# ReLU and row sum on one core: own semaphores, wide instructions, three buffers of 64 KB per partition, and a first load split into 16 and 112 partitions

## Chip, cores, metric

One core of a Trainium2 chip. The metric is device time in microseconds (us); the spans in the profiles are 1.7 to 2.1 us shorter. ACT is the scalar engine, DVE the vector engine, SP the engine that issues the loads. A load (or the chunk of rows that it brings) has landed when the first instruction that waits for it starts. Ratios in this document are the mean time of one kernel's fast runs over the mean of the other's fast runs of the same rounds, so they are not quite the ratios of the medians that are quoted. A run that was timed once is compared with the median of the runs of before on the same chip; such runs carry only differences of several us.

## The reference

```
x: float32 [32, 512, 1024]
relu_x = np.maximum(x, 0)
return np.sum(relu_x, axis=-1)        # [32, 512]
```

That is 16,384 rows of 1,024 elements: 67.1 MB to read, 64 KB to write.

## The kernel before

Each of the 128 partitions gets 128 rows that lie together in memory (512 KB), so a load of 16 rows is 128 runs of 64 KB, 8.4 MB in all. Seven loads of 16 rows go through two buffers. After them come tail loads of 8, 4, 2 and 1 rows, and the last row in four pieces. Each row takes one instruction, on ACT or DVE in turn, which clamps and sums it.

```
big = 16
tail = [8, 4, 2, 1]
io_pool = ctx.enter_context(tc.tile_pool(name="io", bufs=2))
...
for j, cpd in enumerate(chunks):
    xt = io_pool.tile([P, cpd, D], fp32, tag="io", name=f"xt{j}")     # (cut: small tiles have own tags)
    nc.sync.dma_start(out=xt, in_=xv[:, m0 * D : (m0 + cpd) * D].rearrange(...))
    for c in range(cpd):
        ...
        elif (c % 2) == 0:
            act_op(xt[:, c, :], xt[:, c, :], m)       # activation Relu with accum_out
        else:
            dve_op(xt[:, c, :], xt[:, c, :], res[:, m : m + 1])   # tensor_scalar max, add, accum_out
```

The first load is issued ahead of the opening barrier (`EARLY = 1`).

## Time and profile before

| | before |
|---|---|
| median (first three runs) | 163.46 us (163.4 to 163.71) |
| span of the profiled run | 161.5 us |
| busy: DVE, ACT | 46%, 43% |
| 64 KB packet of a load, most of them | 2.42 us |
| first landing; distance of landings | 22.3 us; 19.4 us |

From the page of before: the span, the busy rows, the mean DMA rate and the chain of work that ended last.

```profile
span 161.5 us, 347 instructions
DVE 74.3 (46%) x134; ACT 69.0 (43%) x129; POOL 0.2 (0%) x4
...
DMA  8997997996997997997996997997997997999990
GB/s 308 471 503 308 487 487 308 503 503 292 503 503 308 487 503 325 471 519 308 471 519 296 487 503 325 471 503 341 454 503 341 454 503 308 430 438 406 406 359 22
...
DMA 79%; DVE 18%; SPq 1%; issue 0%; DVEq 0%
```

The chain is DMA. From the timeline of before, the first instruction on each of the first four loads (start in us, length in us, then the idle time before it and what ended it):

```profile
22.26 1.06 ACT L71 ACTIVATE xt<-xt 128x1024 f32<-128x1024 f32 x1 [20.20 <-DMA xt<-in_x_dram]
...
41.61 1.06 ACT L71 ACTIVATE xt<-xt 128x1024 f32<-128x1024 f32 x1 [10.92 <-DMA xt<-in_x_dram]
...
61.04 1.06 ACT L71 ACTIVATE xt<-xt 128x1024 f32<-128x1024 f32 x1 [11.01 <-DMA xt<-in_x_dram]
...
80.39 1.06 ACT L71 ACTIVATE xt<-xt 128x1024 f32<-128x1024 f32 x1 [10.92 <-DMA xt<-in_x_dram]
```

Landings are 19.4 us apart. The packet records in the trace say why. A 16-row load has 128 packets of 64 KB, eight for each of the 16 DMA engines. Sorted by start and taken in groups of 16, one packet per engine, the first groups are:

```
before: group  start us      took ns min/median/max   end us
        0      1.02-2.27     2547/3042/3236           3.97-4.98
        1      3.97-4.98     2418/2418/2472           6.39-7.40
        2      6.38-7.39     2418/2420/2467           8.80-9.81
        7     18.47-19.48    2418/2420/2433          20.90-21.89
        8     20.90-21.90    2418/2418/2418          23.32-24.32   (second load)
```

Each group starts as the one before it ends. No DMA engine waits for a buffer, and eight packets of 2.42 us are the 19.4 us. The alternation in the GB/s row is a matter of counting: the page books a packet, its bytes and its busy time, in the slice where it starts. At 65,536 bytes in 2.42 us, 16 engines move 433 GB/s.

Two idle stretches stand at the front. No packet starts before 1.02 us, and the last DMA engine has its first one only at 2.27 us.

### The profile page before, as it was taken

To read this page: it belongs to the slowest core of one execution; us is meant where nothing else is said; L and a number is where in the kernel's file an instruction comes from. 1 tells how busy PE (TensorE), PEld (TensorE's weight loads), DVE (VectorE), ACT (ScalarE), POOL (GpSimd) and SP (SyncE) were. 2 spreads that over 40 slices of the span, in tenths; PEclk is the share of its full clock that TensorE was granted. 3 is DMA by queue.
4 is the path that set the end of the run, shared out by engine and by line. 5 is a ranking of instruction groups with operands and counts; after the bars stand their busy time and mean duration, and the time that the engine had idled before them with its cause. 6 is when DMAs were issued, how large, how long until landed. Compare 5 with 4: busy or idle time off the path is not lost.

```text
span 161.5 us, 347 instructions
## 1 busy us (share of the span) xinstructions
DVE 74.3 (46%) x134; ACT 69.0 (43%) x129; POOL 0.2 (0%) x4
## 2 busy tenths in 40 slices
DVE  0000049700695008940099101991039900598983
ACT  3000049500693008920099001990039700596882
POOL 0000000000000000000000000000000000000000
DMA  8997997996997997997996997997997997999990
GB/s 308 471 503 308 487 487 308 503 503 292 503 503 308 487 503 325 471 519 308 471 519 296 487 503 325 471 503 341 454 503 341 454 503 308 430 438 406 406 359 22
DMA packets 2450, 67.19 MB, mean 416 GB/s; under 512 B 528, under 2 KB 1040, under 8 KB 1168
## 3 DMA queue, kind: packets, MB, share of 16 engines
q1 hardware_dynamic: 2304, 67.11, 96.9%
q10 hardware_dynamic: 144, 0.06, 0.1%
q14 instruction: 2, 0.02, 0.0%
HBM read 67.11 MB, written 0.07 MB: 416 GB/s over the span
## 4 chain that ended last, share of the span: by engine, by line
DMA 79%; DVE 18%; SPq 1%; issue 0%; DVEq 0%
DMA xt<-in_x_dram 62%; DVE xt L79 17%; DMA p<-in_x_dram 17%; SPq L95 1%; DVE p L79 1%; DVEq L79 0%; DVEq L16 0%
## 5 line engine op out<-in xcount | busy, mean ns | idle before, releaser
L79 DVE TENSOR_SCALAR_CACHE_REDUCE xt<-xt 128x1024 f32<-128x1024 f32 x63 | 72.6, 1216 | 84.5 <-DMA xt<-in_x_dram 84.2
L71 ACT ACTIVATE xt<-xt 128x1024 f32<-128x1024 f32 x64 | 66.7, 1043 | 89.0 <-DMA xt<-in_x_dram 89.0
L71 ACT ACTIVATION_READ_ACCUMULATOR xt<-xt 128x1 f32 x64 | 11.9, 187 | 0.0
L79 DVE DVE_READ_ACCUMULATOR xt<-xt 128x1 f32 x63 | 5.2, 83 | 0.0
L79 DVE TENSOR_SCALAR_CACHE_REDUCE p<-p 128x244 f32<-128x244 f32 (+3 forms) x4 | 1.6, 420 | 0.4 <-DMA p<-in_x_dram 0.4
L71 ACT ACT_TABLE_LOAD x1 | 1.3, 1283 | 0.8 <-PEq L143 0.8
L79 DVE DVE_READ_ACCUMULATOR p<-p 128x1 f32 x4 | 0.3, 82 | 0.0
L143 POOL MEMSET const-bfloat16-1.0<- 128x1 bf16 x1 | 0.1, 101 | 0.0
L143 POOL MEMSET const-uint8-127<- 128x1 uint8 x1 | 0.1, 101 | 0.0
L143 POOL MEMSET const-float32-0.0<- 128x1 f32 x1 | 0.1, 98 | 0.2 <-issue 0.2
L143 POOL MEMSET const-float32-1.0<- 128x1 f32 x1 | 0.1, 98 | 0.0
## 6 DMA issues: line engine op xcount, KB each, us to landing
xt<-in_x_dram SPq DMA_DIRECT2D x1, 4096.0 KB, 19.6
xt<-in_x_dram SPq DMA_DIRECT2D x1, 2048.0 KB, 24.2
xt<-in_x_dram SPq DMA_DIRECT2D x1, 1024.0 KB, 26.2
xt<-in_x_dram SPq DMA_DIRECT2D x1, 512.0 KB, 27.0
p<-in_x_dram SPq DMA_DIRECT2D x1, 134.0 KB, 10.0
p<-in_x_dram SPq DMA_DIRECT2D x1, 130.0 KB, 26.5
p<-in_x_dram SPq DMA_DIRECT2D x1, 126.0 KB, 26.7
p<-in_x_dram SPq DMA_DIRECT2D x1, 122.0 KB, 26.8
```

Of the source, the lines that this page charges most:

```text
L71: nc.scalar.activation(out=out_ap, in_=in_ap, func=mybir.ActivationFunctionType.Relu, accum_out=res[:, m : m + 1],)
L79: nc.vector.tensor_scalar(out=out_ap, in0=in_ap, scalar1=0.0, scalar2=None, op0=mybir.AluOpType.max, op1=mybir.AluOpType.add, accum_out=ac ...
L95: nc.sync.dma_start(out=xt, in_=xv[:, m0 * D : (m0 + cpd) * D].rearrange("p (c d) -> p c d", c=cpd),)
L143: nc = _bacc.Bacc("TRN2", target_bir_lowering=False, num_devices=1)
```

## The change

Its intent, read from the code: give every DMA engine its first packet earlier, with a first load of 16 packets of 64 KB, one per engine, in place of 128 (the split first load), keep one more load in flight (three buffers), and need fewer instructions and semaphore waits (16 or 8 rows per instruction: ACT clamps all of them, then DVE sums all of them). For the last 16-row chunk it goes back to single rows, 10 on ACT and 6 on DVE. The diff, cut to its core:

```
+ROWS = 16
+NBUF = 3
+STEPS = [16, 16, 16, 8, 8, 8]
+ACT_ROWS = 10
+HEADS = 16
-EARLY = 1
+EARLY = 2
...
+    def load(dst, src, after=None, heads=0):
+        if heads:
+            nc.sync.dma_start(out=dst[:heads], in_=src[:heads]).then_inc(sems.loads[n_load], 16)
+            dst, src = dst[heads:], src[heads:]
+        dma = nc.sync.dma_start(out=dst, in_=src)
+        if after:
+            dma.wait_op(sems.dve, after, "sem-ge")
+        dma.then_inc(sems.loads[n_load], 16)
...
+        for c in range(0, ROWS, step):
+            clamp(buf[:, c : c + step, :], ...)                  # ACT: activation Relu
+            total(buf[:, c : c + step, :], m + c, step)          # DVE: tensor_reduce add
...
-        for c in range(cpd):          # one row per instruction
-            (act_op or dve_op)
```

## The prediction

> **What bounds it now: the loads.** The chain that ended last is 79% DMA, 18% DVE; DVE is busy 46% and ACT 43% of the 161.5 us span (page). In the packet records nearly every 64 KB packet takes 2.42 us, and each of the 16 DMA engines starts the next one as the last ends. Eight packets per engine are 19.35 us, and the landings of the 16-row loads (timeline) are just so spaced (22.3, 41.6, 61.0, 80.4, ... 138.9 us). All 67.1 MB at that pace are 154.8 us. The next load is issued 9.3 us after a landing, with 10 us of the other buffer's load left, so two buffers already keep the queue full. Left to win: about 1.1 us until the first packet, 1.2 more until the slowest DMA engine has one, and about 3 us after the last landing.
>
> **What the change does.**
> 1. Three buffers: worth about 0.
> 2. Wide instructions. Now a row costs 1.04 us on ACT or 1.14 on DVE, 16 shared rows 9.2 us. Afterwards each row passes through both. From the 128x1024 and 128x244 DVE rows (1.215 and 0.41 us) DVE takes about 1.03 to 1.04 ns per element[...], so I estimate 17.1 to 17.2 us per 16 rows, 8.6 per 8. [...] Both fit in 19.35, but DVE trails: a chunk's reduce ends 31 us after its landing. From the third landing DVE runs nearly without a pause: [...] 17.2 + 6x8.6 + 13x1.14 + 1.6 = 99 us to its end. The third landing is at 61.0 now, so DVE would end near 160 without the split, against 159.2 now. Buffers are freed 7 us or more before they are needed.
> 3. The split first load should give every DMA engine a packet[...]. The slowest DMA engine gains 0.5 to 1 us on every landing; DVE then ends at about 159.3.
> 4. Own semaphores, one store moved from ACT to SP: about 0.
>
> Gain in front and lateness behind about cancel: 163.3 us.
>
> **Risk.** [...] 7 to 17 us slower. No 16-partition load is in this trace; I give it one in four.
>
> **What would show it.** Head and rest packets: 2.4 to 3.2 us each, first landing at 21 to 22 us[...]. Landings still 19.4 us apart. Reduce groups of 17.1 and 8.6 us[...]. DVE, not the last pieces, on the chain at the tail, starting the row instructions of the seventh chunk about 5 us after that chunk landed.
>
> **What would make it wrong.** [...] a reduce above 19.35 us per 16 rows (DVE becomes the limit); a quicker reduce, with which the tail follows the DMA and the time is near 162.5.
>
> Chances: faster by over 2% 0.03, within 2% 0.70, slower 0.27. Range 162.0 to 169.0.

DVE's sum from the third landing to its end came to 99 us. Its first term, the ACT instruction over 16 rows, is cut; the four terms left add up to 85.2 us. The 31 us to the end of a reduce, the 7 us by which buffers are free early, and all that follows from the 99 us still contain the cut term. (In e1 it took 13.87 us.) The risk came to 7 to 17 us slower. The 7 to 17 us rest on nothing that was measured before the result.

## The result, and the profile after

| | before | after |
|---|---|---|
| median | 163.43 us (4 runs) | 185.2 us (4 runs, 185.01 to 185.9) |
| ratio to before, 95% interval | | 1.134 (1.130 to 1.137) |
| span | 161.5 us | 183.5 us |
| first landing | 22.3 us | 43.5 us |
| last load packet ends | 158.1 us | 178.7 us |

The change costs 21.8 us, and 21.3 of them (43.55 - 22.26) are there when the first chunk has landed. The same lines of the page after:

```profile
span 183.5 us, 152 instructions
DVE 119.5 (65%) x43; ACT 103.8 (57%) x46; POOL 0.2 (0%) x4
...
DMA  9099999979899999999989999999989999899960
GB/s 229 14 214 229 386 257 229 229 229 400 357 428 428 457 457 457 457 443 414 414 357 457 428 457 457 457 457 443 414 371 400 428 457 457 379 436 404 409 230 14
...
DVE 46%; DMA 23%; ACT 23%; another core or an unknown queue 6%; issue 0%; SPq 0%; DVEq 0%
```

Read the two DMA rows together. In the first ten slices (46 us) the DMA engines are nearly always busy, yet they move mostly 229 GB/s (the second slice, 0 and 14, holds few starts of packets). Busy here is a packet under way, not a packet moving at full rate. The chain names DVE and ACT, but that is where the time is at the end. To find where it was lost, compare the landings in the timeline after:

```profile
43.55 13.86 ACT L85 ACTIVATE io<-io 128x16384 f32<-128x16384 f32 x1 [41.01 <-DMA io<-in_x_dram]
...
62.82 13.86 ACT L85 ACTIVATE io<-io 128x16384 f32<-128x16384 f32 x1 [5.41 <-DMA io<-in_x_dram]
...
82.17 13.86 ACT L85 ACTIVATE io<-io 128x16384 f32<-128x16384 f32 x1 [5.50 <-DMA io<-in_x_dram]
```

From the first landing on they are 19.3 us apart again. The packets, in the same groups of 16 as before:

```
after:  group  start us      took ns min/median/max   end us
        0      1.01-1.94     7893/8393/9159           9.13-10.59   (the 16 partitions)
        1      9.13-10.59    4989/5398/5931          14.78-15.63   (the 112 partitions, from here)
        2     14.77-15.62    4701/4718/4866          19.48-20.34
        3     19.48-20.34    2888/3134/4645          22.67-24.80
        7     35.25-37.61    4360/4438/4834          39.62-42.45
        8     39.62-42.45    2687/3318/3567          43.19-45.30   (second load)
        9     43.18-45.30    2418/2420/2426          45.61-47.72
```

The split did what it was meant to do at the very front: the last DMA engine starts at 1.94 instead of 2.27 us. Then all eight packets of each engine are slow. The wide instructions have these lengths (groups by line and form; busy us, mean ns, idle before):

```profile
L93 DVE TENSOR_REDUCE res<-io 128x16 f32<-128x16384 f32 x3 | 51.7, 17221 | 61.6 <-ACT io L85 61.6
L93 DVE TENSOR_REDUCE res<-io 128x8 f32<-128x8192 f32 x6 | 51.6, 8678 | 0.0
L85 ACT ACTIVATE io<-io 128x8192 f32<-128x8192 f32 x6 | 41.9, 7023 | 16.3 <-DMA io<-in_x_dram 16.3
L85 ACT ACTIVATE io<-io 128x16384 f32<-128x16384 f32 x3 | 41.6, 13857 | 51.9 <-DMA io<-in_x_dram 51.9
```

### The profile page after: what moved, and what is told of

Read it like the earlier page. It is cut to its first block, busy times and chain, and to the rows that moved or that the text cites. A ratio compares the mean times of both kernels' runs of the same rounds, so it can differ in the third digit from the quotient of the medians.

```text
span 183.5 us, 152 instructions
## 1 busy us (share of the span) xinstructions
DVE 119.5 (65%) x43; ACT 103.8 (57%) x46; POOL 0.2 (0%) x4
## 4 chain that ended last, share of the span: by engine, by line
DVE 46%; DMA 23%; ACT 23%; another core or an unknown queue 6%; issue 0%; SPq 0%; DVEq 0%
DVE res L93 37%; DMA io<-in_x_dram 23%; ACT io L85 23%; DVE io L110 8%; DVE piece L110 1%; DVE piece L191 0%; SPq L72 0%; DVEq L31 0%
## 5 line engine op out<-in xcount | busy, mean ns | idle before, releaser
L93 DVE TENSOR_REDUCE res<-io 128x8 f32<-128x8192 f32 (+1 forms) x9 | 103.2, 11526 | 61.6 <-ACT io L85 61.6
L85 ACT ACTIVATE io<-io 128x8192 f32<-128x8192 f32 (+1 forms) x9 | 83.4, 9301 | 68.2 <-DMA io<-in_x_dram 68.2
L100 ACT ACTIVATE io<-io 128x1024 f32<-128x1024 f32 x18 | 18.8, 1050 | 5.8 <-DMA io<-in_x_dram 5.7
L110 DVE TENSOR_SCALAR_CACHE_REDUCE io<-io 128x1024 f32<-128x1024 f32 x13 | 14.9, 1220 | 0.0
L100 ACT ACTIVATION_READ_ACCUMULATOR io<-io 128x1 f32 x18 | 3.5, 192 | 0.0
L110 DVE DVE_READ_ACCUMULATOR io<-io 128x1 f32 x13 | 1.2, 89 | 0.0
L110 DVE TENSOR_SCALAR_CACHE_REDUCE piece<-piece 128x244 f32<-128x244 f32 (+2 forms) x3 | 1.1, 416 | 0.0
```

The source lines that it names most:

```text
L85: i = nc.scalar.activation(out=ap, in_=ap, func=RELU)
L93: nc.vector.tensor_reduce(out=res[:, m : m + n], in_=ap, axis=mybir.AxisListType.X, op=ADD).wait_op(sems.act, n_act, "sem-ge").then_inc(se ...
L100: i = nc.scalar.activation(out=ap, in_=ap, func=RELU, accum_out=res[:, m : m + 1])
L110: i = nc.vector.tensor_scalar(out=ap, in0=ap, scalar1=0.0, scalar2=None, op0=MAX, op1=ADD, accum_out=accum_out,)
```

## The experiments

The theory under test is the risk that the prediction had named: that the partitions into which a load goes decide how long its packets take, and that 16 partitions and the other 112 are a bad choice. What the author thought of the path from the DMA engines to the partitions is cut from the expectations, the theory's name and a sharing calculation among it, because no run shows that path; where a cut stands in front of figures, they are those of this theory. They are the author's forecasts, and some of them rested on the cut part. Rivals: the read side (16 rows 512 KB apart in memory), something about short or odd-sized loads in themselves, two DMAs for one chunk, or the rest of the change. "Write side" in the expectations is the side of the destination partitions.

### e1: the change without the split

```
-HEADS = 16        -EARLY = 2
+HEADS = 0         +EARLY = 1
```

> The changed kernel with its first load left whole (and one load ahead of the barrier, as before). [...] (the split alone costs the 22 us[...]): 163.4 to 164.8 us, first landing at 22.3 us, packets of 2.42 us, DVE row instructions of the seventh chunk 5 us after its landing, end 0.5 to 1.4 us later than before. Rival (wide instructions or the third buffer slow the loads): still 175 us or more.

Measured: 164.17 us (5 runs), ratio 1.005 (1.0035 to 1.006). First landing at 22.28 us. Packets are 2.42 us after the first group.

```profile
22.28 13.86 ACT L85 ACTIVATE io<-io 128x16384 f32<-128x16384 f32 x1 [20.22 <-DMA io<-in_x_dram]
```

So 21 of the 22 us belong to the split (`EARLY` was changed with it; e7 has `EARLY = 2` and no loss). Wide instructions and the third buffer together neither slow the loads nor speed them up (landings at 22.28 and, the third, 61.01 us, against 22.26 and 61.04 before).

The remaining 0.7 us are at the tail. The end of the chain in order of time (start us, us, what):

```profile
41.66 13.86 ACT io L85
...
61.01 13.87 ACT io L85
74.87 0.02 issue
74.90 68.78 DVE res L93 x7
143.67 14.57 DVE io L110 x25
...
159.53 0.44 DVE piece L191
```

ACT clamps the third chunk from its landing at 61.01 on. From 74.90 DVE pauses for no more than 0.16 us at a time, and it ends at 159.97, 98.96 us after that landing. The prediction had added up 99 us and "near 160 without the split".

### e2: before, with only the split

```
+        if j == 0:
+            nc.sync.dma_start(out=xt[:16], in_=src[:16])
+            nc.sync.dma_start(out=xt[16:], in_=src[16:])
+        else:
+            nc.sync.dma_start(out=xt, in_=src)
-EARLY = 1
+EARLY = 2
```

> The kernel before with only its first load split into 16 and 112 partitions, both ahead of the barrier. [...] 183 to 186 us, first landing near 43 us as in the changed kernel, later landings 19.4 us apart. Rival (the rest of the change is needed for the loss): 163 to 166 us.

Measured: 184.53 us (4 runs), ratio 1.127 (1.126 to 1.129), landings:

```profile
44.37 1.22 DVE L79 TENSOR_SCALAR_CACHE_REDUCE xt<-xt 128x1024 f32<-128x1024 f32 x1 [44.37 <-DMA xt<-in_x_dram]
63.61 1.06 ACT L71 ACTIVATE xt<-xt 128x1024 f32<-128x1024 f32 x1 [9.59 <-DMA xt<-in_x_dram]
...
83.03 1.06 ACT L71 ACTIVATE xt<-xt 128x1024 f32<-128x1024 f32 x1 [11.00 <-DMA xt<-in_x_dram]
```

The split alone costs 21.1 us (184.53 - 163.47). With the 0.7 us of e1 that is the whole 21.8.

### e3, e4, e8, e10, e11, e12: one extra load of 16 partitions

These runs put one unused load of 1 MB first in the queue of the kernel before. The two loads ahead of the barrier are then this one and the first real one. Only the destination partitions and the source rows differ:

```
+    spare = io_pool.tile([P, big, D], fp32, tag="io", name="spare")
+    nc.sync.dma_start(out=spare[0:16], in_=xv[0:16, 0 : big * D]...)      # e3
#                      out=spare[0:106:7]                                  # e4
#                      out=spare[32:93:4]                                  # e11
#                      out=spare[11:117:7]                                 # e12
#                      in_=x_flat[0 : 16 * big, :]...                      # e8 (as e4), e10 (as e3): 1 MB together
```

e3: 

> The kernel before plus one unused 1 MB load of 16 partitions into partitions 0 to 15, first in the queue. [...] its packets take 8 to 9.7 us, everything else moves by 9 to 10 us, about 173 us. Rival (a 16-partition load is nothing special): packets of 2.4 to 3.2 us, about 166 us.

e4: 

> The same extra load from the same rows of the input, but into every seventh partition (0, 7, ... 105)[...]. [...] (the write side decides): packets of 2.4 to 6 us, everything moves by 4 to 6 us[...], about 168 us. Rival (the read side decides: 16 rows 512 KB apart in memory, or the short 16-descriptor load itself): the same as with partitions 0 to 15, about 173 us.

e8: 

> The extra load of 16 partitions into every seventh partition again, but reading 1 MB that lies together in memory instead of 16 rows 512 KB apart. In the run with the far rows all 16 packets took 4.0 to 5.4 us[...]. If the read side caused that, packets of 2.4 to 3.2 us now[...] and about 166 to 167 us; if the write side did[...], 4 to 5.4 us again and 168 us.

e10: 

> The extra load into partitions 0 to 15 again, reading 1 MB that lies together in memory. Write side decides: 172 to 173 us and packets of 8 to 9 us as with the far rows. Read side has a part in it: less, 166 to 170 us.

e11: 

> The extra load of 16 partitions, far rows, into partitions 32, 36, ... 92[...]. [...] packets of 2.4 to 3.2 us, everything moves by the 2.4 us of its data, 165.6 to 166.3 us. If a 16-partition load is slow in itself, 168 us or more.

e12: 

> The extra load, far rows, into partitions 11, 18, ... 116[...]. [...] 2.4 to 3.2 us and 166 us, like step 4. [...] (what the 4 us packets of the step-7 run suggest): packets of 4 us or more and 167.5 to 168.5 us.

Measured, one timed run each. "Cost" is the time less the median of before (163.46 to 163.49 us). "Packets" are the 16 packets of the extra load, shortest and longest.

| run | partitions | source rows | time us | cost us | packets us |
|---|---|---|---|---|---|
| e3 | 0 to 15 | 512 KB apart | 172.63 | 9.2 | 7.7 to 9.3 |
| e10 | 0 to 15 | together | 172.71 | 9.3 | 7.8 to 9.1 |
| e4 | 0, 7, ... 105 | 512 KB apart | 168.13 | 4.7 | 4.0 to 5.4 |
| e8 | 0, 7, ... 105 | together | 168.00 | 4.5 | 3.7 to 5.0 |
| e12 | 11, 18, ... 116 | 512 KB apart | 166.27 | 2.8 | 2.5 to 3.3 |
| e11 | 32, 36, ... 92 | 512 KB apart | 166.07 | 2.6 | 2.7 to 3.3 |

Where the first real load lands, in the timeline of e11, e12, e4 and e3, in this order:

```profile
24.62 1.06 ACT L71 ACTIVATE xt<-xt 128x1024 f32<-128x1024 f32 x1 [21.73 <-DMA xt<-in_x_dram]
```

```profile
24.66 1.06 ACT L71 ACTIVATE xt<-xt 128x1024 f32<-128x1024 f32 x1 [21.74 <-DMA xt<-in_x_dram]
```

```profile
27.14 1.06 ACT L71 ACTIVATE xt<-xt 128x1024 f32<-128x1024 f32 x1 [24.23 <-DMA xt<-in_x_dram]
```

```profile
31.11 1.06 ACT L71 ACTIVATE xt<-xt 128x1024 f32<-128x1024 f32 x1 [28.58 <-DMA xt<-in_x_dram]
```

The same megabyte costs 2.6 or 9.2 us, and only the destination partitions decide it. In e11 and e12 it costs about what its data must (2.6 and 2.8 us, where one packet takes 2.42), so a 16-partition load is not slow in itself. The read side has no part that these runs can see: near and far rows agree within 0.2 us (e3 and e10, e4 and e8). Nor is the spacing of the partitions the reason: e4 and e12 have the same step of 7 and differ only in where they start (their packets, 4.0 to 5.4 and 2.5 to 3.3 us, do not overlap). In e3 the megabyte takes from 1.01 to 10.48 us, which is 111 GB/s, about four times the 27 GB/s of one engine (65,536 bytes in 2.42 us), where 16 engines in a whole load move 433.

My doubt after e4 rested on which engine takes which partition, and the trace does not tell that. Had it been right, e12's packets would have taken 4 us or more. e12 does not bear it out: they took 2.5 to 3.3 us, about as long as in e11. What makes 11, 18, ... 116 a better choice than 0, 7, ... 105, where all 16 packets took at least 3.7 us, stays open; the runs show only that the read side is not the reason.

### e5: one extra load of the other 112 partitions

```
+    nc.sync.dma_start(out=spare[16:128], in_=xv[16:128, 0 : big * D]...)
```

> The kernel before plus one unused 7.3 MB load of 112 partitions (16 to 127), first in the queue. Seven packets per engine at 2.42 us would be 16.9 us. [...] ([...]it must account for what the 16-partition load, 6.8 us dearer than its data, leaves of the 21 us): everything moves by about 31 us, 193 to 196 us[...]. Rival (only the 16-partition head hurts): plus 17 us, 180 us.

Measured: 193.88 us, one timed run, a cost of 30.4 us where seven packets at 2.42 us would be 16.9. The first real load lands here:

```profile
53.35 1.06 ACT L71 ACTIVATE xt<-xt 128x1024 f32<-128x1024 f32 x1 [50.80 <-DMA xt<-in_x_dram]
```

The medians of its seven groups of packets run from 3.0 to 4.8 us. So the larger part of the split is the dearer one: 30.4 - 16.9 = 13.5 us over its data, against 9.2 - 2.6 = 6.6 us for the head. Their sum, 20.1 us, is close to the 21.1 of e2.

The packets differ in the course of the load. In order, the medians of the groups are 4.78, 4.65, 2.99, 3.71, 4.47, 4.60 and 4.44 us. In each of the two quick groups, the third and the fourth, exactly two packets take 4.4 to 4.7 us and the other 14 take 2.8 to 3.7. Why the groups differ, no run shows.

### e6 and e7: splitting in equal halves, by partitions and by rows

```
e6:  -HEADS = 16   +HEADS = 64
e7:  -HEADS = 16   +HEADS = 8
     -  out=dst[:heads], in_=src[:heads]          +  out=dst[:, :heads], in_=src[:, :heads]
     -  dst, src = dst[heads:], src[heads:]       +  dst, src = dst[:, heads:], src[:, heads:]
```

e6: 

> The changed kernel with its first load split into 64 and 64 partitions. [...] packets of about 4.8 us, first landing at 40 us or somewhat later, 183 to 188 us. Rival (odd sizes hurt, equal powers of two do not): near 164 us.

e7: 

> The changed kernel with its first load split by rows, 8 rows and 8 rows of all 128 partitions, both ahead of the barrier. [...] no loss[...], packets of 1.2 us, first landing at 22.3 us, 163.9 to 164.6 us. Rival (two DMAs for one chunk, or two DMAs ahead of the barrier, cost by themselves): over 166 us.

Measured: e6 185.31 us (one timed run), e7 164.26 us (4 runs, ratio 1.0045, 1.003 to 1.006). The first landings, e6 and then e7:

```profile
43.51 13.86 ACT L85 ACTIVATE io<-io 128x16384 f32<-128x16384 f32 x1 [40.40 <-DMA io<-in_x_dram]
```

```profile
22.37 13.86 ACT L85 ACTIVATE io<-io 128x16384 f32<-128x16384 f32 x1 [19.82 <-DMA io<-in_x_dram]
```

In e6 nearly all packets of the first load take 4.7 to 5.1 us, about twice the usual 2.42, through both halves. An even split by partitions is as bad as 16 and 112 (185.31 us against 185.2). Two DMAs for one chunk, both ahead of the barrier, cost nothing here when each has all 128 partitions (e7's ratio is 1.0045, that of e1 with one DMA 1.005). Nor do they gain anything: the last DMA engine of e7 has its first packet at 2.49 us, no earlier than before.

### e9: no split, 11 rows of the seventh chunk on ACT

```
-ACT_ROWS = 10     -HEADS = 16    -EARLY = 2
+ACT_ROWS = 11     +HEADS = 0     +EARLY = 1
```

> The changed kernel with its first load whole and 11 instead of 10 rows of the seventh chunk on ACT. If the 0.7 us by which the whole-load version is slower than before is DVE's lateness at the tail (it began that chunk's rows 5.2 us after the landing and ended last), a row less for DVE gives about 1.1 us back: 162.8 to 163.3 us, level with before or just under it. If the 0.7 us lies elsewhere (end of the program, later landings): 163.9 to 164.4 as without the change of rows.

Measured: 163.43 us (6 runs, one of them 164.32), ratio 1.001 (0.999 to 1.003): level with before. The end of its chain:

```profile
143.67 13.67 DVE io L110 x24
157.34 0.89 DVE piece L110 x5
...
158.38 0.43 DVE piece L191
```

DVE ends at 158.81 instead of 159.97 us, so the row moved gave back 1.16 us in the profile, as expected. The measured time gave back less, 0.7 us (164.17 to 163.43; the spans of e9 are 2.0 to 2.1 us shorter than its times, those of e1 1.8), and missed the expected 162.8 to 163.3 by 0.1 us. So DVE's lateness accounts for the 0.7 us of e1, while the 0.3 us that e9 takes more outside its span stay unexplained. This is the best version that the experiments lead to, and it does not beat before.

## Why the prediction was wrong, point by point

- **What bounds the kernel: right.** Packets follow each other without a gap. The third buffer brought no landing forward (third landing at 61.01 us in e1, 61.04 before). It was not tested apart from the wide instructions, and these probably need it: a 16-row chunk is done 13.86 + 17.22 = 31.1 us after its landing, while the load already queued lasts 19.4 us, so with two buffers the DMA engines would have to wait about 12 us (an estimate from these numbers, not run).
- **Wide instructions: right.** Predicted 17.1 to 17.2 and 8.6 us for DVE, measured 17.22 and 8.68; 17.22 us for 16,384 elements is 1.05 ns each, where the prediction had 1.03 to 1.04. ACT measured 13.86 and 7.02, which is 0.834 ns for each of the 8,192 further elements. DVE was to begin the seventh chunk's rows 5 us after the landing; it began at 164.76, after a landing that ACT saw at 159.57. DVE's lateness without the split: predicted "near 160" for its end, measured 159.97 (e1).
- **The step that failed** is the third: the split first load was to give every DMA engine its first packet earlier, and "the slowest DMA engine gains 0.5 to 1 us on every landing". The first half holds in a smaller size: the slowest engine starts 0.33 us earlier (1.94 us against 2.27). The second does not: the first landing comes 21.3 us later, and the last packet of a load still ends 20.6 us later. What the step had wrong was the length of the packets: it counted on "head and rest packets" of 2.4 to 3.2 us each. The 16 partitions took 7.9 to 9.2 us per packet (e3, e11 and e12 show that the partitions decide it), the 112 partitions 3.1 to 5.4 (group medians; e5 shows the cost of this part, but no run shows why it is slow).
- **The risk was named and weighed wrongly.** The loss came where it said, and I gave it one in four. I had no measurement for it and none against it. What held me back, as I remember it (the prediction says only that no such load was in the trace), was that somebody had put the split there, and intent is no measurement.
- **Its size was too small as well.** "7 to 17 us slower" did not hold (21.1 in e2). The load's last packet ended 41.4 us after its first began (42.45 - 1.01); before, it was 20.9 us (21.89 - 1.02). The head alone took 9.5 us in e3 (10.48 - 1.01). The larger part is the 112-partition load, 13.5 us over its data (e5). Why some choices of partitions make the packets of all engines slow, and how an engine's seven partitions are chosen, stays open.

## What to carry to other kernels

Split a load by rows within the partitions (e7, first landing at 22.37 us), not into ranges of partitions (e2 and e6, 44.37 and 43.51): in the ranges tried here (0 to 15, 16 to 127, 0 to 63 and 64 to 127) nearly all packets took longer than the 2.42 us of a whole load, and the engines show as busy all the while. In a profile the sign is a full DMA row over a low GB/s row (in after mostly 9 over mostly 229 GB/s in the first ten slices), and packets of the same size that take up to nearly four times as long (here 9.2 us instead of 2.42). When the loads already run without gaps, the most that a change at the front can win is the time until the slowest engine's first packet, here 2.3 us; weigh a known risk of many us against that before trusting the intent.
